# Gate and norm columns turned into rows through TensorE and 512-byte runs in DRAM, with the loads placed later

## The chip, the cores and the metric

One core of a Trainium2 chip runs the kernel. The metric is the device time of one execution in microseconds (us), and each kernel is run several times. TensorE (PE) does the matrix products and the transposes, VectorE (DVE) and ScalarE (ACT) the element work, GpSimd (POOL) a few powers, and SyncE (SP) issues every DMA of this kernel, in order, from one queue. An instruction that must wait holds up everything behind it on its engine.

## The reference, cut to what matters

A two-layer diffusion trunk: 512 latent tokens and 256 context tokens of 1024 channels, in float32. Layer 0 mixes tokens by attention, layer 1 by pooling, and each is followed by a gated feed-forward with 2816 hidden channels.

```python
m = (sc @ w_mod[i] + b_mod[i]).reshape(B, N_MOD, D_MODEL)
shift_m, scale_m, gate_m, shift_f, scale_f, gate_f = [m[:, k] for k in range(N_MOD)]
h = modulate(rmsnorm(x, g_pre_mix[i]), shift_m, scale_m)          # h * (1 + scale) + shift
...                                                                # mixer: y
x = x + gate_m * rmsnorm(y, g_post_mix[i])
h = modulate(rmsnorm(x, g_pre_ffn[i]), shift_f, scale_f)
x = x + gate_f * rmsnorm(conv_ffn(h, w_up[i], conv_w[i], conv_b[i], w_down[i]), g_post_ffn[i])
```

The vectors m have 1024 entries for each layer. The change concerns how five products of them, all functions of the channel alone, get from one layout to another.

## The kernel before, in words

Each float32 product is made of three matmuls on high and low parts (`mm3`, L122 to L124). The parts of a weight come from a 512 KB load into a `raw` buffer (two of them), a cast on ACT (L128, `whi`) and a subtraction on DVE (L129, `wlo`), with five buffers for each part.

A modulation vector is computed in eight chunks of 128 channels (`mod_chunk`): a 512 KB load of `w_mod` on SP (L184) and one reduction of the load on DVE (L186), which leaves the chunk as a column of `mods`, channel p of the chunk on partition p. These chunks are background work: a list `bg`, from which `background(n)` pops n steps at places in the attention, in the first up-projection (`up`) and in the first down-projection (`down` with `each0`). After the last chunk of a gate, `gate_col` multiplies the column by the norm's gain into `Gcol`; `gain_col` makes `Acol` in the same way.

A pre-norm on transposed data uses the columns as they are. A post-norm (`post_norm`, L247) works with tokens on partitions and needs the 1024 channels as a row on every partition. `to_row` (L203) does that: it stores the 128 x 8 column to DRAM with its two dimensions exchanged (L206), so that neighbouring channels, which lie on different partitions, come to lie side by side, and loads the 1024 channels back, the same row to all 128 partitions (L207). It is called five times in the code for `Grow`, `Gm1`, `Arow` and `Brow`, and once more for the last `Grow`:

- L481, in the attention, for `Grow` of the first post-norm;
- L790, in the first up-projection, for `Grow` of the first feed-forward;
- L907, at the step c = 0, kk = 10 of the first down-projection, for `Gm1` (it lies in `cvt`, the buffer of the up-projection's activations), followed by `pool_bias`;
- L910 and L911, at c = 1, kk = 5, for `Arow` and `Brow`, in slots that hold gated activations until then;
- L932, after the second up-projection (`up7`), for `Grow` of the last post-norm.

`pool_bias` (L808) loads `psr` and two rows of `bpr`, multiplies them on DVE (L815) and splits the product (L816, L817). A down-projection has two halves c of the output channels; for each of 11 weight blocks kk it multiplies four token tiles t, into bank `B2[t][c]`.

The order of the code isn't the order on the engines. A planner takes the code's instructions, follows their dependencies in a model of time and issues on each engine the earliest ready one, so that a step stands where the model finds its inputs and its buffer free, often long ahead of its place in the code. The order so found is fixed in the program.

Of the kernel before, what the change touches and what calls it, by code (L numbers as in the profile page):

```python
# [11 lines left out]
F32 = mybir.dt.float32  # L12
# [5 lines left out]
P = 128  # L18
D = 1024
SEQ = 512  # L20
CTX = 256
KT = D // P
# [9 lines left out]
FT = DFF // P  # L32
# [17 lines left out]
def trunk(ctx: ExitStack, tc: tile.TileContext, a, out: bass.AP):  # L50
    nc = tc.nc
    V, S, G, T = nc.vector, nc.scalar, nc.gpsimd, nc.tensor
# [7 lines left out]
    dram = ctx.enter_context(tc.tile_pool(name="dram", bufs=2, space=bass.MemoryType.DRAM))  # L60
# [23 lines left out]
    def flat(z):  # L84
        return z.rearrange("p a b -> p (a b)")
# [8 lines left out]
    ident = const.tile([P, P], F32, name="ident")  # L94
# [13 lines left out]
    mods = const.tile([P, 2, 6, KT], F32, name="mods")  # L108
    cmods = const.tile([P, 2, KT], F32, name="cmods")
    Acol = const.tile([P, 2, 2, KT], F32, name="Acol")  # L110
    Acx = const.tile([P, KT], F32, name="Acx")
    Gcol = const.tile([P, 2, 2, KT], F32, name="Gcol")
    scrow = rows("scrow", 60)
    Grow = big.tile([P, D], F32, name="Grow")
    cvt = slots("cvt", 62, 2, F32)
    h32 = big.tile([P, KT, P], F32, name="h32")
# [29 lines left out]
    def row_tile(name):  # L146
        return work.tile([P, D], F32, tag="row", name=name)
# [34 lines left out]
    def mod_chunk(i, v, j):  # L182
        raw = mraw[0]()
        nc.sync.dma_start(out=raw, in_=a["w_mod"][i, v, j])  # L184
        bias = bmod[:, i, v, j:j + 1]
        V.tensor_tensor_reduce(raw, raw, scrow, 1.0, bias, ALU.mult, ALU.add, mods[:, i, v, j:j + 1])  # L186

    def mod_vector(i, v, then=None):
        def last():
            mod_chunk(i, v, KT - 1)  # L190
            if then is not None:
                then()
        return [lambda j=j: mod_chunk(i, v, j) for j in range(KT - 1)] + [last]

    def gain_col(i, n):

        V.scalar_tensor_tensor(Acol[:, i, n, :], mods[:, i, 3 * n + 1, :], 1.0, gcols[:, n, i, :],
                               op0=ALU.add, op1=ALU.mult)

    def gate_col(i, n):  # L200
        V.tensor_mul(Gcol[:, i, n, :], mods[:, i, 3 * n + 2, :], gcols[:, 2 + n, i, :])

    def to_row(dst, col):  # L203

        d = dram.tile([KT, P], F32, tag="bounce", name="bounce")
        nc.sync.dma_start(out=d.rearrange("j p -> p j"), in_=col)  # L206
        nc.sync.dma_start(out=dst, in_=d.rearrange("j p -> (j p)").unsqueeze(0).broadcast_to([P, D]))  # L207

    bg = []

    def background(n):
        for _ in range(min(n, len(bg))):
            bg.pop(0)()


    hT = slots("hT", 0, 2 * KT)
# [77 lines left out]
    cols = small.tile([P, KT, 2], F32, name="cols", bufs=1)  # L294
# [50 lines left out]
    for j in range(KT):  # L345
# [5 lines left out]
        if j % 2 == 0:  # L351
            i = 28 + 2 * j
            wkv.append(load_w(a["w_qkv"][2, j // 2], 2, (rows(f"wkvh{j}", i, dt=F32R), rows(f"wkvl{j}", i + 2, dt=F32R))))
        f = slice(j * P, (j + 1) * P)
# [123 lines left out]


    mraw[0] = lambda: wp.tile([P, 1024], F32, tag="raw", name="mraw", bufs=2)  # L480
    bg += mod_vector(0, 2, lambda: (gate_col(0, 0), to_row(Grow, Gcol[:, 0, 0, :])))  # L481
    bg += mod_vector(0, 3) + mod_vector(0, 4, lambda: gain_col(0, 1))

    banks.close()
# [13 lines left out]
    def tp_next():  # L498
        tp_n[0] += 1
        return tp_ps[tp_n[0] % 2]  # L500
# [55 lines left out]
    for i in range(len(heads) + DEPTH):  # L556
# [4 lines left out]
        if i < len(heads):  # L561
# [8 lines left out]
            elif len(wo) < 8:  # L570
                n = len(wo)
# [7 lines left out]
        if i == len(heads) + 1:  # L579
# [3 lines left out]
            B2 = [[z[:, :512], z[:, 512:]] for z in W2]  # L583
# [14 lines left out]
    B2 = [[z[:, :512], z[:, 512:]] for z in W2]  # L598
# [39 lines left out]

    SPLIT = 4

    def up7(i, a32, mid, tail, early=2):

# [20 lines left out]
        load = lambda f: [load_w(a["w_up"][i, f, n], KT) for n in range(2)]  # L665
# [71 lines left out]
        for f in range(SPLIT, FT + 1):  # L737
            g = f - 1 if f > SPLIT else None
            new = f < FT
            if new:  # L740
                if f == SPLIT:
                    weights(f)
                row = row_tile("gates")
                rows_of[f] = (row[:, :512], row[:, 512:768])
                af, bc = A[(f - SPLIT) % 4], W2[f % 2]
                prod(af[:, :256], f, 1, True)
                S.copy(row[:, 0:256], af[:, :256])
            if g is not None:
                ag, bg_ = A[(g - SPLIT) % 4], W2[g % 2]
                gate, s5 = rows_of.pop(g)  # L750
                prod(ag[:, :256], g, 7, False)
                V.tensor_add(ag[:, 256:], ag[:, :256], s5)
            if new:
                prod(bc[:, :256], f, 2, True)
            if g is not None:
                prod(bg_[:, 512:768], g, 3, False)
                g2 = gate.rearrange("p (a b) -> p a b", a=2)
                V.tensor_add(g2, bg_.rearrange("p (a b) -> p a b", a=2)[:, :, :256], g2)
                act(g, gate)
            if new:  # L760
                prod(af[:, :256], f, 6, False)
                S.copy(row[:, 256:512], af[:, :256])  # L762
            if g is not None:
                prod(ag[:, :256], g, 4, False)
                V.scalar_tensor_tensor(a32[g], ag, -1.0, a32[g], op0=ALU.mult, op1=ALU.mult)
                W.pop(g)
            if new:
                prod(bc[:, 512:768], f, 5, True)
                S.copy(row[:, 512:768], bc[:, 512:768])
            if f + 1 < FT:  # L770
                weights(f + 1)
            if f >= FT - 3:
                tail(f - FT + 3)

    LAST = 6
    EARLY = FT - 2 * LAST
# [10 lines left out]

    a0 = gated("a0")
    mraw[0] = lambda: row_tile("mraw")
    bg += mod_vector(0, 5, lambda: (gate_col(0, 1), to_row(Grow, Gcol[:, 0, 1, :])))  # L790
    bg += mod_vector(1, 0) + mod_vector(1, 1, lambda: gain_col(1, 0))
    bg += mod_vector(1, 2, lambda: gate_col(1, 0))
    bg += mod_vector(1, 3) + mod_vector(1, 4, lambda: gain_col(1, 1))
# [4 lines left out]
    Gm1 = flat(cvt)  # L798
    hall = slots("hall", 52, KT, F32)
    wpl_dst = [[rows(f"wpl{n}{z}", i + 2 * z, dt=F32R) for z in range(2)] for n, i in enumerate((16, 20))]  # L800
    Arow, Brow = rows("Arow", 24), rows("Brow", 26)
# [6 lines left out]
    def pool_bias():  # L808

        ps, b = row_tile("psr"), row_tile("bpr")  # L810
        nc.sync.dma_start(out=ps, in_=a["pool_scale"].broadcast_to([P, D]))
        V.memset(b, 0.0)
        nc.sync.dma_start(out=b[0:1, :], in_=a["b_pool"])
        nc.sync.dma_start(out=b[32:33, :], in_=a["b_pool"])
        V.tensor_mul(b[0:33, :], b[0:33, :], ps[0:33, :])  # L815
        S.copy(bp, b)  # L816
        V.tensor_sub(bp[32:33, :], b[32:33, :], F(bp[32:33, :]))  # L817
        return ps
# [47 lines left out]
    def mixed(t):  # L866
        pre_norm(t, B2[t], mixrow[t], Acol[:, 1, 1], mods[:, 1, 3], hall[:, :, t * P:(t + 1) * P])
# [29 lines left out]
            mix(2)  # L897
            mix(3)

    ps_row = []  # L900

    def each0(c, kk):
        background(2)
        if c == 0 and kk == 8:
            background(100)
        if c == 0 and kk == 10:
            to_row(Gm1, Gcol[:, 1, 0, :])  # L907
            ps_row.append(pool_bias())
        if c == 1 and kk == FT // 2 - LAST:
            to_row(Arow, Acol[:, 1, 0, :])  # L910
            to_row(Brow, mods[:, 1, 0, :])  # L911
            pool_weights(ps_row[0])

    def down(i, aT, done, each, last, dst=(), order=(2, 3, 0, 1)):
# [8 lines left out]
    a32 = [place(f"a32{f}", gated_slot(1, f), (512,), F32) for f in range(FT)]  # L923
# [4 lines left out]
            for half in range(2):  # L928
                split(a1[half][f][:, 0, :], a1[half][f][:, 1, :], a32[f][:, half * 256:(half + 1) * 256])

    up7(1, a32, lambda: (mixed(2), mixed(3)), split_pair)
    to_row(Grow, Gcol[:, 1, 1, :])  # L932

    def finish(t):
        row = row_tile("outrow")
# [91 lines left out]
```

## Time and profile before

| | |
|---|---|
| median of 3 runs | 1067.87 us (1063.73 to 1069.53) |
| the profiled execution | 1074.04 us, its span 1072.3 us |
| granted TensorE clock, mean | 0.977 of full speed |
| PE busy | 997.8 us, 93% of the span |
| DVE busy | 747.6 us, 70% |
| ACT busy | 511.4 us, 48% |
| DMA moved | 143.70 MB in 46778 packets, 11122 of them under 512 bytes |

The stages of the span: modulation, the first pre-norm and the key, value and query products to about 110 us; attention to about 300 us; the first up-projection to about 544 us, the first down-projection to about 660 us; pooling mixer to about 720 us; then the second feed-forward. In the traces a line "start, length, engine, line" is an instruction or several merged ones; the bracket behind it gives how long its engine was idle before it and what ended that.

### The profile page before, as it was taken

What the parts mean: (1) busy time and instruction counts of PE and PEld (TensorE: products, weight loads), DVE (VectorE), ACT (ScalarE), POOL (GpSimd) and SP (SyncE); (2) the same over time, 40 slices, a digit from 0 to 9 for tenths busy, and PEclk for the clock granted to TensorE, in tenths of its full rate; (3) what the DMA queues carried; (4) which work ended last, traced back from release to release, by engine and by line L of the source; (5) the groups of instructions that cost most, each with busy time, mean ns of one, the idle gap of its engine ahead of it and who ended that gap; (6) DMA issues with size and microseconds to landing.
All of it is one profiled execution on the core that took longest, in us unless ns stands there. A gap on an engine that the chain in (4) does not pass through costs nothing.

```text
span 1072.3 us, 14605 instructions
## 1 busy us (share of the span) xinstructions
PE 997.8 (93%) x5586; PEld 862.9 (80%) x5586; DVE 747.6 (70%) x1259; ACT 511.4 (48%) x986; POOL 37.5 (3%) x55
## 2 busy tenths in 40 slices
PE   0898889999979999989999999899999999999997
PEld 0666678788878888878888887788999999988885
DVE  3988777896777999565542236889799999982214
ACT  5658578865624333244331223555455555761111
POOL 2003000000000000000000001110000000000000
PEclk9999899999989999989999999989999999999999
DMA  8543431352189989744333353411132332043312
GB/s 316 193 150 98 154 92 70 118 159 77 40 274 247 335 316 338 134 104 138 98 114 102 99 180 106 133 45 40 60 118 81 118 107 91 21 157 99 99 59 78
DMA packets 46778, 143.70 MB, mean 134 GB/s; under 512 B 11122, under 2 KB 11506, under 8 KB 46708
## 3 DMA queue, kind: packets, MB, share of 16 engines
q1 hardware_dynamic: 46708, 142.77, 41.4%
q8 instruction: 43, 0.70, 0.3%
q14 instruction: 27, 0.22, 0.1%
HBM read 140.63 MB, written 2.12 MB: 133 GB/s over the span
## 4 chain that ended last, share of the span: by engine, by line
PE 56%; DVE 18%; DMA 12%; ACT 8%; issue 4%; POOL 2%; SPq 0%; DVEq 0%; ACTq 0%; POOLq 0%
PE b L124 11%; PE b L122 11%; PE b L123 11%; PE b L733 5%; DMA mraw<-in_w_mod 5%; PE b L734 5%; DVE mraw L186 5%; PE b L735 5%; DVE wlo L129 3%; DMA raw<-in_w_up 2%; POOL rr L151 2%; DMA bpr<-in_b_pool 1%; DMA bounce<-Gcol 1%; DMA raw<-in_w_o 1%; DVE x L254 1%
## 5 line engine op out<-in xcount | busy, mean ns | idle before, releaser
L129 DVE TENSOR_TENSOR wlo<-raw,whi 128x1024 fp32r<-128x1024 f32 x105 | 128.0, 1223 | 150.2 <-ACT whi L128 150.0
L128 ACT CAST whi<-raw 128x1024 fp32r<-128x1024 f32 x105 | 110.1, 1053 | 178.9 <-PE b L124 105.1
L122 PE MATMUL b<-hT,whi 128*128 128x512 f32 (+1 forms) x480 | 175.5, 367 | 7.4 <-ACT hT L128 5.2
L123 PE MATMUL b<-hT,whi 128*128 128x512 f32 (+1 forms) x480 | 175.5, 366 | 0.6 <-DVE hT L129 0.6
L124 PE MATMUL b<-hT,wlo 128*128 128x512 f32 (+1 forms) x480 | 175.4, 366 | 0.6 <-DVE wlo L129 0.6
L122 PE MATMUL b<-whi,a 128*128 128x512 f32 x320 | 124.6, 390 | 0.8 <-ACT whi L128 0.8
L123 PE MATMUL b<-wlo,a 128*128 128x512 f32 x320 | 124.6, 389 | 0.3 <-DVE wlo L129 0.3
L124 PE MATMUL b<-whi,a 128*128 128x512 f32 x320 | 124.4, 389 | 0.0
L186 DVE CUSTOM_DVE_ANT_0 mraw<-mraw,scrow,bmod 128x1024 f32<-128x1024 f32 x80 | 101.2, 1281 | 14.8 <-DMA mraw<-in_w_mod 14.6
L122 PEld LDWEIGHTS b<-hT,whi 128*128 128x128 f32 x480 | 92.4, 193 | 22.3 <-ACT hT L128 5.6
L124 PEld LDWEIGHTS b<-hT,wlo 128*128 128x128 f32 x480 | 92.4, 193 | 15.1 <-DVE wlo L129 1.3
L123 PEld LDWEIGHTS b<-hT,whi 128*128 128x128 f32 x480 | 92.4, 192 | 15.0 <-DVE hT L129 1.1
L733 PE MATMUL b<-hT,whi 128*128 128x256 f32 x288 | 81.9, 285 | 0.1
L735 PE MATMUL b<-hT,wlo 128*128 128x256 f32 x288 | 81.5, 283 | 0.0
L734 PE MATMUL b<-hT,whi 128*128 128x256 f32 x288 | 81.4, 283 | 0.0
L151 POOL TENSOR_TENSOR rr<-rv,mhalf 128x1 f32<-128x1 f32 (+2 forms) x48 | 36.7, 768 | 1029.4 <-DVE rv L169 854.6
L122 PEld LDWEIGHTS b<-whi,a 128*128 128x128 f32 x320 | 60.0, 188 | 13.9 <-ACT whi L128 1.2
L123 PEld LDWEIGHTS b<-wlo,a 128*128 128x128 f32 x320 | 60.1, 188 | 13.3 <-DVE wlo L129 0.7
L124 PEld LDWEIGHTS b<-whi,a 128*128 128x128 f32 x320 | 60.1, 188 | 12.2
L733 PEld LDWEIGHTS b<-hT,whi 128*128 128x128 f32 x288 | 55.2, 192 | 1.0 <-ACT gates L762 0.9
L734 PEld LDWEIGHTS b<-hT,whi 128*128 128x128 f32 x288 | 55.2, 192 | 0.0
L735 PEld LDWEIGHTS b<-hT,wlo 128*128 128x128 f32 x288 | 55.2, 192 | 0.0
(307 smaller groups left out, 2162.4 us busy)
## 6 DMA issues: line engine op xcount, KB each, us to landing
mraw<-in_w_mod SPq DMA_DIRECT2D x96, 512.0 KB, 5.1
raw<-in_w_up SPq DMA_DIRECT2D x52, 512.0 KB, 4.0
raw<-in_w_down SPq DMA_DIRECT2D x44, 512.0 KB, 3.4
upv<-in_w_up SPq DMA_DIRECT2D x18, 512.0 KB, 4.1
upg<-in_w_up SPq DMA_DIRECT2D x18, 512.0 KB, 3.5
raw<-in_w_qkv SPq DMA_DIRECT2D x12, 512.0 KB, 4.3
raw<-in_w_o SPq DMA_DIRECT2D x8, 512.0 KB, 3.5
x<-in_x SPq DMA_DIRECT2D x4, 512.0 KB, 10.0
```

The costliest lines, as they stand in the source:

```text
L122: T.matmul(ps, lh, rh, start=first, stop=False)
L123: T.matmul(ps, lh, rl, start=False, stop=False)
L124: T.matmul(ps, ll, rh, start=False, stop=last)
L128: S.copy(hi, src)
L129: V.tensor_sub(lo, src, F(hi))
L151: G.tensor_tensor(r[:, :n], v, mhalf[:, :n], op=ALU.pow)
L186: V.tensor_tensor_reduce(raw, raw, scrow, 1.0, bias, ALU.mult, ALU.add, mods[:, i, v, j:j + 1])
L254: V.scalar_tensor_tensor(xc, row[:, HALVES[c]], r, xc, op0=ALU.mult, op1=ALU.add)
L733: T.matmul(ps, lhs[0], rhs[0], start=first and k == 0, stop=False, skip_group_check=True)
L734: T.matmul(ps, lhs[0], rhs[1], start=False, stop=False, skip_group_check=True)
L735: T.matmul(ps, lhs[1], rhs[0], start=False, stop=last, skip_group_check=True)
```

## The change

`to_row` is replaced by `to_rows`. It takes one or more columns, transposes each on TensorE into eight rows of 128 channels in a PSUM bank, copies these with ACT into part of the tile `h32`, and stores them to DRAM so that each run is 512 bytes. It returns the loads as functions, and the callers place them. The load of the first row stands at least three background steps after its store in the code (`later`). The other five columns are made at one place, c = 0, kk = 10 of the first down-projection, four in one store and one in another, through the banks `B2[0][1]` and `B2[1][1]`. The loads of `Grow` and `Gm1` stand at c = 1, kk = 2, those of `Arow` and `Brow` where they stood, and the last load of `Grow` in the middle of `up7`.

```diff
-    def to_row(dst, col):
-
-        d = dram.tile([KT, P], F32, tag="bounce", name="bounce")
-        nc.sync.dma_start(out=d.rearrange("j p -> p j"), in_=col)
-        nc.sync.dma_start(out=dst, in_=d.rearrange("j p -> (j p)").unsqueeze(0).broadcast_to([P, D]))
-
-    bg = []
+    def to_rows(ps, cols):
+
+        n = len(cols)
+        for c, col in enumerate(cols):
+            T.transpose(ps[0:KT, c * P:(c + 1) * P], col, ident)
+        stage = h32[0:KT, 0:n, :]
+        S.copy(stage, ps[0:KT, :n * P].rearrange("j (n p) -> j n p", n=n))
+        d = dram.tile([n, KT, P], F32, tag="bounce", name="bounce")
+        nc.sync.dma_start(out=d.rearrange("n j p -> j n p"), in_=stage)
+        return [lambda dst, c=c: nc.sync.dma_start(
+            out=dst, in_=d[c].rearrange("j p -> (j p)").unsqueeze(0).broadcast_to([P, D])) for c in range(n)]
+
+    bg, later = [], []
 
     def background(n):
         for _ in range(min(n, len(bg))):
             bg.pop(0)()
+            if later:
+                later[0][0] -= 1
+                if later[0][0] < 0:
+                    later.pop(0)[1]()
...
-    bg += mod_vector(0, 2, lambda: (gate_col(0, 0), to_row(Grow, Gcol[:, 0, 0, :])))
+
+    def mix_gate():
+        gate_col(0, 0)
+        load, = to_rows(tp_next(), [Gcol[:, 0, 0, :]])
+        later.append([3, lambda: load(Grow)])
+
+    bg += mod_vector(0, 2, mix_gate)
...
+            if f == FT // 2:
+                midway()
...
-    bg += mod_vector(0, 5, lambda: (gate_col(0, 1), to_row(Grow, Gcol[:, 0, 1, :])))
+    bg += mod_vector(0, 5, lambda: gate_col(0, 1))
...
         if c == 0 and kk == 10:
-            to_row(Gm1, Gcol[:, 1, 0, :])
+            row_loads.extend(to_rows(B2[0][1], [Gcol[:, 0, 1, :], Gcol[:, 1, 0, :], Acol[:, 1, 0, :], mods[:, 1, 0, :]]))
+            row_loads.extend(to_rows(B2[1][1], [Gcol[:, 1, 1, :]]))
             ps_row.append(pool_bias())
+        if c == 1 and kk == 2:
+            row_loads[0](Grow)
+            row_loads[1](Gm1)
         if c == 1 and kk == FT // 2 - LAST:
-            to_row(Arow, Acol[:, 1, 0, :])
-            to_row(Brow, mods[:, 1, 0, :])
+            row_loads[2](Arow)
+            row_loads[3](Brow)
             pool_weights(ps_row[0])
...
-    up7(1, a32, lambda: (mixed(2), mixed(3)), split_pair)
-    to_row(Grow, Gcol[:, 1, 1, :])
+    up7(1, a32, lambda: (mixed(2), mixed(3)), split_pair, lambda: row_loads[4](Grow))
```

## Rows read from the trace of the kernel before

**Rows 1.** The page: busy time by engine; PE's busy tenths in 40 slices of 26.8 us

```profile
PE 997.8 (93%) x5586; PEld 862.9 (80%) x5586; DVE 747.6 (70%) x1259; ACT 511.4 (48%) x986; POOL 37.5 (3%) x55
...
PE   0898889999979999989999999899999999999997
```

**Rows 2.** Windows, attention: stretch, its length, busy time by engine, granted clock, DMA, GB/s

```profile
145.00:150.00 5.00, 5.00 (x31) 4.27 (x30) 4.24 (x11) 4.02 (x15) 1.01 (x1) 1.00 0.20 26
150.00:155.00 5.00, 4.44 (x33) 3.87 (x32) 1.45 (x4) 4.17 (x10) 0.00 (x0) 1.00 0.75 233
155.00:160.00 5.00, 0.39 (x2) 0.40 (x3) 2.67 (x6) 0.00 (x0) 0.00 (x0) 0.87 0.25 48
160.00:165.00 5.00, 5.00 (x18) 4.13 (x17) 2.32 (x7) 3.19 (x7) 0.00 (x0) 0.50 0.23 90
165.00:170.00 5.00, 5.00 (x35) 4.37 (x35) 2.45 (x5) 2.43 (x5) 0.00 (x0) 0.94 0.02 5
```

**Rows 3.** Timeline of SP in the attention: start, length, line, transfer

```profile
139.15 0.39 SPq L206 DMA_DIRECT2D bounce<-Gcol  x1
140.29 0.34 SPq L133 DMA_DIRECT2D raw<-in_w_o  x1
151.09 0.33 SPq L207 DMA_DIRECT2D Grow<-bounce  x1
151.51 0.38 SPq L184 DMA_DIRECT2D mraw<-in_w_mod  x1
```

**Rows 4.** Timelines of DVE and PE behind that, with the idle time before each

```profile
157.32 1.28 DVE L186 CUSTOM_DVE_ANT_0 mraw<-mraw,scrow,bmod 128x1024 f32<-128x1024 f32 x1 [5.87 <-DMA mraw<-in_w_mod]
...
159.61 0.90 PE L525 MATMUL tp<-ident,p 128*128 128x128 f32 x3 [5.17 <-DVE qT L129]
```

**Rows 5.** DMA issues of 139 to 152 us: transfer, count, KB, median us to landing

```profile
raw<-in_w_o SPq DMA_DIRECT2D x1, 512.0 KB, 12.0
```

**Rows 6.** Line 206, all six stores: from issue to landing

```profile
DMA to landing us min/median/max: 10.8/13.5/17.0
```

**Rows 7.** Timeline of SP in the first up-projection

```profile
435.35 0.44 SPq L206 DMA_DIRECT2D bounce<-Gcol  x1
...
446.54 0.38 SPq L206 DMA_DIRECT2D bounce<-Gcol  x1
447.01 0.43 SPq L813 DMA_DIRECT2D bpr<-in_b_pool  x1
```

**Rows 8.** Timeline of DVE behind that

```profile
461.78 1.22 DVE L815 TENSOR_TENSOR bpr<-bpr,psr 33x1024 f32<-33x1024 f32 x1 [13.76 <-DMA bpr<-in_b_pool]
```

**Rows 9.** Windows, first up-projection, columns as in the second group

```profile
463.00:466.00 3.00, 0.82 (x4) 0.40 (x3) 2.46 (x4) 2.97 (x5) 0.00 (x0) 0.99 0.00 0
466.00:470.00 4.00, 3.42 (x8) 2.15 (x8) 3.80 (x5) 1.33 (x3) 0.00 (x0) 0.50 0.40 116
470.00:480.00 10.00, 10.00 (x40) 8.11 (x39) 6.77 (x10) 5.96 (x10) 0.00 (x0) 0.86 0.51 163
```

**Rows 10.** Windows around the second store of line 206, same columns

```profile
310.00:320.00 10.00, 7.03 (x35) 6.86 (x36) 8.88 (x16) 3.58 (x7) 0.00 (x0) 0.54 0.84 274
320.00:330.00 10.00, 10.00 (x76) 9.59 (x75) 6.78 (x11) 1.74 (x3) 0.00 (x0) 1.00 1.06 206
```

**Rows 11.** Timeline of SP, last load of Grow

```profile
684.89 0.33 SPq L207 DMA_DIRECT2D Grow<-bounce  x1
```

**Rows 12.** Tile tp: a line's durations min/median/max in ns, first and last start

```profile
L525 PE MATMUL tp<-ident,p x192: 270/272/477, 124.3 to 290.9; 128*128 128x128 f32 x192
```

**Rows 13.** DMA issues after 1050 us, stores of the output

```profile
out_x<-x SPq DMA_DIRECT2D x8, 256.0 KB, 2.0
```

**Rows 14.** Waits of SP's queue, 540 to 640 us: total, times, longest

```profile
SPq L133 <- DVE wlo L129: 66.0, 14, 5.4
```

**Rows 15.** Timeline of ACT in the first down-projection

```profile
600.46 1.06 ACT L128 CAST whi<-raw 128x1024 fp32r<-128x1024 f32 x1 [4.38 <-PE b L124]
```

**Rows 16.** Windows, first down-projection, columns as in the second group

```profile
600.00:610.00 10.00, 10.00 (x45) 8.26 (x44) 2.45 (x2) 2.11 (x2) 0.00 (x0) 1.00 0.23 73
```

More of the change, by code (lines that the diff above doesn't have):

```diff
@@ L639, in trunk, with up7 @@
     SPLIT = 4
-    def up7(i, a32, mid, tail, early=2):
+    def up7(i, a32, mid, tail, midway, early=2):
         def act(f, gate):
@@ L898, in after_ffn0 @@
             mix(3)
-    ps_row = []
+    ps_row, row_loads = [], []
     def each0(c, kk):
```

## The prediction

> **What bounds the kernel now.** PE is busy for 93% of the span [rows 1], so a stall elsewhere costs time only where PE runs dry behind it. I therefore looked first at where the change works, the stores and loads of L206 and L207 on SP, then at what stood behind each on SP, then at DVE and PE there, and last at the windows, which say whether PE stopped and what its clock was afterwards.
>
> Two places show a chain from such a store to an idle PE. The first is in the attention. The store of `Gcol` goes out at 139.15, a weight load at 140.29, and then the queue stands until 151.09, when the load of `Grow` may read what was stored; only then does the next `mraw` load go, at 151.51 [rows 3]. DVE has that chunk next in its order and is idle for 5.87 us until it lands; PE needs what DVE does after it and is idle for 5.17 us [rows 4]. When PE resumes, it does so at half clock, the lower of its two levels, for about five microseconds [rows 2].
>
> The second is in the up-projection. Three stores go out from 435.35 on and a fourth at 446.54, right ahead of the two small `bpr` loads [rows 7]. Those are 4 KB each, yet DVE waits for them for 13.76 us, until 461.78 [rows 8], and its weight parts are missing when PE gets to them: PE is idle between 463 and 470 and at half clock again [rows 9].
>
> What makes the stores slow? The six land 10.8 to 17.0 us after their issue [rows 6], while 256 KB of output in longer runs land in 2.0 us [rows 13]. The 512 KB weight load issued 1.1 us behind the first store takes 12.0 us [rows 5], although only 26 GB/s move in the meantime [rows 2]. So a store in 4-byte pieces (1024 of them) holds up whatever is queued behind it for some 11 us, not because the DMA engines are full of bytes. I take the piece length as the cause.
>
> **The change, part by part.** Sums go against the profiled execution (span 1072.3 us, 1074.0 with what lies around it), which is 6.2 us above the median of the runs; I carry that difference over.
>
> *First store and load (attention).* The wait of SP goes. Without it `mraw` can be issued shortly after 140.3 instead of 151.5 and land before DVE asks for it at 151.4 (157.32 less 5.87). Gain, from the windows [rows 2]: idle PE 0.56 + 4.61 = 5.2 us, and of the clock 5.0 x (1 - 0.50) + 5.0 x (1 - 0.94) = 2.8 us, together 8.0 us. What is late next: PE was full at 145 to 150 with DVE at 4.24 of 5 us [rows 2], so PE should stay the limit.
>
> What comes in is a longer chain: `Gcol`, a transpose on PE, a copy on ACT, the store. PE and ACT wait in order for it, and behind the store on SP stand the weight load and `mraw`. The transpose is 0.27 us [rows 12], the copy about half of the 1.06 us that a cast of 1024 columns takes [rows 15], plus what stands ahead of it on ACT. The new store's landing isn't in the trace; bounds are 2.0 [rows 13] and 17.0 us [rows 6]. I take 2.0, since its runs are 512 bytes and it has 8 of them. SP is then free for `mraw` at about 143.5 even if the load stands right behind the store; the slack until DVE starves is 151.4 - 5.8 (landing of this `mraw`) = 145.6, so 2 us remain. Cost: nothing, and the 8.0 us come back in part if that slack is used up.
>
> *Later loads.* The planner moves steps: the last `Grow` store of the code stands after the second up-projection and goes out at 446.54 [rows 7], its load at 684.89 [rows 11], as soon as its buffer is free. So the delays written into the code may hold on no engine. I count nothing for them, neither for the first load nor for the one in `up7`: the first needs no delay at a landing of 2 us, and the last ran ahead without one.
>
> *Second store (feed-forward gate, 322 us).* PE is full at full clock behind it [rows 10], so its removal is worth nothing, and the cover is PE's own work; the idle time before 320 precedes the store.
>
> *The four stores at 435 to 447.* They can't stay there. Their transposes go into banks that the up-projection's last two blocks still use, so they can't run before those have been read, shortly ahead of 544 us, where that stage ends. Then nothing slow stands ahead of `bpr`, DVE's 13.76 us shrink to the few microseconds of a small load, and the weight parts are in time. Gain [rows 9]: idle 2.18 + 0.58 = 2.8 us, clock 3.42 x 0.50 + 10.0 x 0.14 = 3.1, together 5.9 us. Behind it PE is busy for 90% or more of each of the next seven slices, 482 to 670 us [rows 1], so the gain is kept.
>
> *Five transposes, two copies, two stores in the down-projection.* PE is full there [rows 16], so its work adds: the transposes cost 0.27 us each alone [rows 12] and less in a row, where they overlap (three took 0.90 us even at half clock [rows 4]); with the one in the attention I take 1.2 us for six. By the Trainium skill ("TensorE: Matmul & The Clock Gate", part 4) one takes about 275 ns in a kernel, so 1.65 us for six, an estimate; the row has the same duration, and the difference is only their overlap. The copies, 0.6 us each, lie in ACT's 4.38 us of idle time per weight [rows 15].
>
> A wait is added: both copies use the same part of `h32`, so the second, on ACT, waits until the first store has landed, and PE's first product into `B2[1][1]` waits for that copy. The store may itself stand behind a weight load that waits up to 5.4 us [rows 14]. Worst: 5.4 + 2.0 + 0.6 = 8.0 us, less the tile in between (6 matmuls at 10.0 us for 45 [rows 16], 1.3 us) = 6.7 us idle, plus 3 us of clock as in the other two gaps. Best: nothing, where the planner puts the other tiles or weight blocks ahead. ACT's casts behind the waiting copy are four weights ahead of PE, so they don't suffer. I take 1 us, near the lower end, since the planner knows this wait and PE has other ready work.
>
> **Sum.** 1074.0 - 8.0 - 5.9 + 1.2 + 1.0 = 1062.3 us, less 6.2 = 1056 us against the median of 1067.9.
>
> **The rivals.** *One gap stays.* In the attention DVE waits for `mraw` at other times too, and PE now waits for the transpose; the gap may only shrink. With the second gap alone: 1067.9 - 5.9 + 2.2 = 1064; with the first alone 1062. For it: the slack of 2 us. Against it: the stall has one clear head. I give 1063.
>
> *Given back.* PE also stops at 300 to 320, with the clock down to 0.54 [rows 10]. That stretch waits for modulation chunks and a norm, and work that arrives earlier may just wait longer there: 8 us of the first gap are lost, partly the second: 1066.
>
> *The store stays slow.* If the landing doesn't come from the pieces but from the write to DRAM or from what is queued, the new one takes 10.8 to 17.0 us as well. Then the first gap stays, the second goes, and the wait in the down-projection is 5.4 + 13.5 + 0.6 - 1.3 = 18 us of idle PE, with 3 of clock: 1067.9 - 5.9 + 1.2 + 18 to 21 = 1081 to 1084 at worst, about 1076 with a part covered by reordered tiles. With both gaps gone it decides from about 10 us of idle PE at that place (10 + 3 = 13.9 - 1.2). Against it: 2.0 us [rows 13] for a store to DRAM. The Trainium skill ("DMA: Bandwidth & Descriptors", Bandwidth) goes by size: 4 KB take 0.68 us and all under 64 KB is dominated by descriptors, there on GpSimd's path. Taken by size alone the old store's 10.8 us would have to be queueing, and this rival would hold; the count of descriptors, 1024 against 8, is the reading that the rows bear out.
>
> *It doesn't do what it says.* The loads aren't later, as argued; at a landing up to about 4 us this gives the same 1056 to 1058.
>
> **How the numbers follow.** Forecast, with the last rival: 0.62. One gap stays: 0.18. Given back: 0.11. Store stays slow: 0.09. A measurement of this kernel tells apart about 0.5%, 5.3 us; faster means under 1062.5. That is the forecast and about half of the second case: 0.70; slower 0.09; the rest, 0.21, within. The range: the low end is all of 13.9 us without the costs, less the 4 us by which single runs lie below the median: 1050. The high end is the third case, 1066, which also takes in the worst of the added wait (9.7 us in place of 1).
>
> **What would show it.** Right: SP without a stand of 10 us behind `bounce`, landings of 2 to 4 us, DVE L186 without the 5.87 us, L815 with under 4 us, no clock of 0.50 at either place. Wrong: `bounce` landings over 5 us; a PE wait on ACT between the two halves of the down-projection; a new DVE wait for `mraw`; more idle time at 300 to 320.

## The result and the profile after

The kernel after takes 1057.35 us (1056.28 to 1059.54, six runs), the kernel before on the same chip 1068.74 us (1063.73 to 1072.84, six runs): a ratio of 0.9898 [0.9871, 0.9926]. Measured again later, beside the last experiment, it was 1057.51 against 1073.33 us, 0.9852 [0.9825, 0.9879]. The profiled execution of after takes 1057.91 us with a span of 1056.1 us, 16.1 us less than that of before.

The page of after: engines, the granted clock in 40 slices of 26.4 us, and packets. Beside [rows 1] PE has 7 us less of busy time for six more instructions, and the packets under 512 bytes are 4906 where they were 11122:

```profile
PE 990.8 (94%) x5592; PEld 857.4 (81%) x5592; DVE 747.5 (71%) x1259; ACT 512.9 (49%) x989; POOL 37.4 (4%) x55
...
PEclk9999899999989999999999999899999999999999
...
DMA packets 40611, 143.71 MB, mean 136 GB/s; under 512 B 4906, under 2 KB 5338, under 8 KB 40540
```

Windows of after, with the columns of [rows 2]: the attention, the first up-projection and the first down-projection. They answer to [rows 2, 9 and 16]:

```profile
140.00:150.00 10.00, 10.00 (x70) 9.07 (x69) 8.61 (x20) 8.41 (x25) 1.01 (x1) 1.00 0.31 104
150.00:160.00 10.00, 10.00 (x69) 8.77 (x69) 6.83 (x15) 7.74 (x16) 0.00 (x0) 1.00 0.18 54
160.00:170.00 10.00, 10.00 (x65) 8.87 (x64) 8.53 (x18) 9.88 (x28) 1.01 (x1) 1.00 0.08 18
...
450.00:460.00 10.00, 10.00 (x46) 8.29 (x45) 4.47 (x7) 4.03 (x6) 0.00 (x0) 1.00 0.30 102
460.00:470.00 10.00, 10.00 (x46) 8.29 (x45) 4.43 (x7) 4.01 (x6) 0.00 (x0) 1.00 0.32 105
...
600.00:610.00 10.00, 10.00 (x45) 8.27 (x45) 3.68 (x3) 1.05 (x1) 0.00 (x0) 1.00 0.72 261
```

Both gaps are gone: PE is full in both places and the granted clock stays at its upper level. In the third place, where the change added its work, PE is full too.

The timeline of SP in after (start, length, line, transfer) answers to [rows 3 and 7]:

```profile
138.87 0.33 SPq L133 DMA_DIRECT2D raw<-in_w_o  x1
142.51 0.33 SPq L184 DMA_DIRECT2D mraw<-in_w_mod  x1
...
180.83 0.35 SPq L211 DMA_DIRECT2D bounce<-h  x1
182.07 0.35 SPq L212 DMA_DIRECT2D Grow<-bounce  x1
...
595.35 0.30 SPq L211 DMA_DIRECT2D bounce<-h  x1
...
598.23 0.32 SPq L211 DMA_DIRECT2D bounce<-h  x1
598.61 0.33 SPq L212 DMA_DIRECT2D Grow<-bounce  x1
```

No store stands at 139 or at 435 to 447 any more. `mraw` goes out 3.6 us behind the weight load, where it was 11.2 us. The first store goes only at 180.83, and the load that reads it follows 1.24 us later: the store has landed by then. DVE's steps that waited, in its timeline of after, start without an idle time ahead of them, where [rows 4 and 8] show 5.87 and 13.76 us:

```profile
149.94 1.28 DVE L186 CUSTOM_DVE_ANT_0 mraw<-mraw,scrow,bmod 128x1024 f32<-128x1024 f32 x1
...
428.45 1.21 DVE L833 TENSOR_TENSOR bpr<-bpr,psr 33x1024 f32<-33x1024 f32 x1
```

The new work, in the timelines of PE and of ACT in after: the first transpose, one of the later five, and the second copy, behind its wait for the first store of the down-projection.

```profile
179.01 0.27 PE L207 MATMUL tp<-ident,Gcol 128*8 128x128 f32 x1
...
593.82 0.27 PE L207 MATMUL b<-ident,Acol 128*8 128x128 f32 x1
```

```profile
596.91 0.26 ACT L209 COPY h<-b 8x128 f32<-8x128 f32 x1 [0.63 <-DMA bounce<-h]
```

To see where the time went I took the start of the same instructions out of the traces: the transposes of p in the attention (L525 of before), products of the first up- and down-projection, and the mixer's products with `band`. Times of before in us, then each kernel's difference to it; the kernels e1 to e10 are those of the next section, and e8 is before once more:

```
                     before   after     e1     e2     e3     e6     e7     e8     e9    e10
p-transpose 32       147.54   -1.43  -4.33  -1.52  -1.27  -1.77  -1.73  -1.46  -4.06  -2.35
p-transpose 64       178.90   -9.32 -12.24  -3.62  -9.18  -1.63  -3.73  -3.08 -11.96 -10.24
p-transpose 128      221.71  -11.28 -12.00  -3.48  -5.04  -1.62  -5.52  -3.18 -12.06 -11.70
up-proj. product 500 397.16  -11.34 -12.54  -3.96  -7.13  -1.48  -7.72  -3.52 -11.88 -11.51
first down-proj.     551.12  -17.53 -11.21 -10.14 -13.31  -7.66 -13.31  -3.01 -18.06 -17.69
band first           656.71  -17.34 -11.24  -9.24 +11.35  -7.75 -10.88  -1.38 -17.74 -17.04
band last            692.09  -15.90 -11.25  -9.26 +11.35  -6.32  -7.88  -1.37 -16.30 -17.05
end                 1072.26  -16.13  -9.85  -7.38 +10.67  -5.23  -8.96  -1.69 -15.86 -15.70
```

A difference below zero is an earlier start; what a kernel wins in a stretch is what its difference falls by from one line to the next. After wins 7.9 us between the 32nd and the 64th transpose, the place of the first gap, and 2.0 more by the 128th; nothing between 222 and 397 us; 6.2 in the place of the second gap. It loses 0.2 us over the down-projection and 1.4 in the pooling mixer.

### The profile page after: what moved, and what is told of

Read it like the earlier page. It is cut to its first block, busy times and chain, and to the rows that moved or that the text cites. A ratio compares the mean times of both kernels' runs of the same rounds, so it can differ in the third digit from the quotient of the medians.

```text
span 1056.1 us, 14619 instructions
## 1 busy us (share of the span) xinstructions
PE 990.8 (94%) x5592; PEld 857.4 (81%) x5592; DVE 747.5 (71%) x1259; ACT 512.9 (49%) x989; POOL 37.4 (4%) x55
## 2 busy tenths in 40 slices
DMA packets 40611, 143.71 MB, mean 136 GB/s; under 512 B 4906, under 2 KB 5338, under 8 KB 40540
## 4 chain that ended last, share of the span: by engine, by line
PE 75%; DVE 8%; ACT 7%; DMA 5%; issue 3%; POOL 2%; SPq 0%; DVEq 0%; ACTq 0%; POOLq 0%
PE b L122 16%; PE b L124 16%; PE b L123 16%; PE b L749 6%; PE b L751 5%; PE b L750 5%; DMA mraw<-in_w_mod 2%; POOL rr L151 2%; PE tp L541 1%; DVE wlo L129 1%; DVE mraw L186 1%; ACT whi L128 1%; DVE x L264 1%; DMA raw<-in_w_up 1%; PE sc L122 1%
```

## The experiments

Ten experiments ran, e1 to e4, e5 to e8, and e9 with e10 each beside one another on one chip, with runs of before between them. Lines are numbered by each kernel's own code.

**The first row alone.** The kernel after, with the other five columns stored as before:

```diff
+    def to_row(dst, col):
...
-    bg += mod_vector(0, 5, lambda: gate_col(0, 1))
+    bg += mod_vector(0, 5, lambda: (gate_col(0, 1), to_row(Grow, Gcol[:, 0, 1, :])))
...
+            to_row(Gm1, Gcol[:, 1, 0, :])
...
+            to_row(Arow, Acol[:, 1, 0, :])
+            to_row(Brow, mods[:, 1, 0, :])
...
+    to_row(Grow, Gcol[:, 1, 1, :])
```

> Only the first row (Grow of the attention's post-norm) goes through TensorE and a 512-byte store; the other five columns are stored in 4-byte pieces as before. Theory (two separate gaps, each with its own store): the gap at 150 to 170 us goes, the one at 463 to 480 stays, 8 us below the kernel before, about 1061; DVE L186 without the wait of 5.87 us, DVE L815 with its 13 to 14 us. Rival (one gap stays where work is given back): within 3 us of before.

It took 1064.69 us (1058.88 to 1068.37, ten runs), a ratio to before of 0.9932 [0.9905, 0.9959]. In its windows the first gap is gone, and the second is there, larger than in [rows 9]:

```profile
150.00:160.00 10.00, 10.00 (x66) 8.56 (x65) 5.85 (x12) 7.74 (x23) 0.00 (x0) 1.00 0.12 48
...
450.00:455.00 5.00, 0.96 (x5) 0.46 (x3) 2.39 (x3) 1.65 (x4) 0.00 (x0) 0.79 0.24 16
455.00:460.00 5.00, 3.60 (x8) 2.47 (x9) 4.93 (x7) 2.58 (x4) 0.00 (x0) 0.52 0.25 70
```

Its list of waits (total, times, longest) has 17.0 us of DVE for `bpr`, where [rows 8] has 13.76:

```profile
DVE bpr L839 <- DMA bpr<-in_b_pool: 17.0, 1, 17.0
...
PE b L122 <- ACT whi L128: 5.6, 2, 5.0
```

So one part of the gain stands without the other; the wait for `bpr` is within what before itself shows (17.5 us in its second profile, below). Between the 500th product and the down-projection this kernel loses 1.3 us to before's first profile, where before's second loses 0.5: at most a part of what the first gap brings is waited off in the second, as long as that is there.

**The other rows alone.** The kernel after, with the first column stored as before:

```diff
+    def to_row(dst, col):
...
-        load, = to_rows(tp_next(), [Gcol[:, 0, 0, :]])
-        later.append([3, lambda: load(Grow)])
+        to_row(Grow, Gcol[:, 0, 0, :])
```

> The first row is stored in 4-byte pieces as before; the other five columns go through TensorE in the first down-projection. Theory: the wait of SP of about 10 us in the attention stays with 5 us of idle PE and 5 us of half clock behind it; no slow store stands ahead of bpr; 5.9 us for that gap, less nearly nothing for the added work, so about 6 us below the kernel before, 1062 to 1063. The sum of this gain and that of the run with the first row alone is that of the whole change, 11.4 us, within 2. Rival (added work in the down-projection costs 2 us): 4 us below.

1066.83 us (1063.12 to 1068.40, ten runs), a ratio of 0.9944 [0.9918, 0.9970]. SP stands again between store and load, the waits are those of [rows 4], and the windows show the first gap and a full PE in the place of the second:

```profile
137.64 0.39 SPq L218 DMA_DIRECT2D bounce<-Gcol  x1
...
149.38 0.33 SPq L219 DMA_DIRECT2D Grow<-bounce  x1
```

```profile
155.00:160.00 5.00, 2.85 (x11) 2.46 (x12) 4.50 (x9) 2.27 (x4) 0.00 (x0) 0.76 0.33 105
...
420.00:480.00 60.00, 60.00 (x266) 49.69 (x265) 36.75 (x52) 23.03 (x34) 0.00 (x0) 1.00 0.36 116
```

The two parts give 8.3 and 6.1 us by the medians beside before's 1072.95. Their sum, 14.4, is 3.0 us more than the 11.4 that the expectation allowed 2 us around. It lies between the 11.4 and the 15.8 us that the whole change gave in its two measurements, so within what before itself varies they add up.

**The same kernel with its stores in 4-byte pieces.** The kernel after, in which only the order of the numbers in DRAM is another, so that each store falls into pieces of one number and the rows hold their channels in another order; the transposes, copies, loads and their order on every engine are those of after:

```diff
-        d = dram.tile([n, KT, P], F32, tag="bounce", name="bounce")
-        nc.sync.dma_start(out=d.rearrange("n j p -> j n p"), in_=stage)
+        d = dram.tile([n, P, KT], F32, tag="bounce", name="bounce")
+        nc.sync.dma_start(out=d.rearrange("n p j -> j n p"), in_=stage)
...
```

> The changed kernel with one thing other: the three stores write the same elements in 4-byte pieces (1024, 4096 and 1024 of them) in place of 512-byte runs, so the loaded rows have their channels in another order; all engines have the same instructions in the same order. Theory (the number of pieces sets the landing, about 11 us for 1024, and holds up the queue behind): the first store lands 11 us or later, SP stands for that long at 181 us and PE stops there as it did at 154; the second takes some 45 us, the weights of the down-projection come late by more than the four that are ahead (22 us), and PE is idle there for 20 us or more: 25 to 45 us slower than the changed kernel. Rival (the new place and the late loads are what helps, not the length of the runs): within 3 us of the changed kernel.

1084.80 us (1084.11 to 1088.58, four runs): 27 us above after, and slower than before, 1.0141 [1.0098, 1.0185]. The first store, 1024 pieces from eight partitions, holds SP from 181.01 to 189.02, 8.0 us:

```profile
181.01 0.34 SPq L211 DMA_DIRECT2D bounce<-h  x1
189.02 0.35 SPq L212 DMA_DIRECT2D Grow<-bounce  x1
```

The second, of 4096 pieces, is what the second copy waits for, and PE waits for that copy, as the list of waits and the windows show:

```profile
ACT h L209 <- DMA bounce<-h: 21.5, 1, 21.5
...
PE b L122 <- ACT h L209: 19.7, 1, 19.7
```

```profile
600.00:610.00 10.00, 2.60 (x12) 1.81 (x10) 1.54 (x2) 0.49 (x1) 0.00 (x0) 0.73 0.45 3
610.00:620.00 10.00, 0.00 (x0) 0.00 (x0) 0.00 (x0) 0.00 (x0) 0.00 (x0) 0.50 0.75 25
620.00:630.00 10.00, 7.74 (x28) 6.31 (x29) 2.45 (x2) 1.31 (x2) 0.00 (x0) 0.74 0.50 87
```

The expectation missed the sizes, 11 and 45 us where 8.0 and about 22 were measured, and the path: it had PE run out of weights, and PE waited for the copy. By the table the two stores cost 6.1 us (64th to 128th transpose, -9.18 to -5.04, where after goes from -9.32 to -11.28) and 24.5 us (first down-projection to `band`, +24.66, where after has +0.19). Of the 6.1 us, about 4.1 are left by the 500th product (-7.13 beside -11.34).

**The loads at once.** The kernel after without the delays of its loads:

```diff
-        later.append([3, lambda: load(Grow)])
+        load(Grow)
...
-    up7(1, a32, lambda: (mixed(2), mixed(3)), split_pair, lambda: row_loads[4](Grow))
+    up7(1, a32, lambda: (mixed(2), mixed(3)), split_pair, lambda: None)
+    row_loads[4](Grow)
```

> The changed kernel with its loads directly behind their stores in the code, the last one behind the second up-projection as before, so without the delays. Theory (the planner places them by their buffers, and the short store lands in under 2 us): same time as the changed kernel within 1 us, with the first load at the same place on SP. Rival (the delays matter): SP stands behind a store, and up to 8 us of the gain are lost.

1058.90 us (1058.77 to 1059.53, four runs), 0.9894 [0.9848, 0.9941]; the first load goes out at 182.13, in after at 182.07. The median is 1.4 to 1.6 us above the two of after, which ran beside other runs of before; the ratios to before agree, so the delays do nothing here that can be measured.

**Runs of 64 bytes.** The kernel after with stores in runs of 16 numbers, eight times as many as in after; here too the rows hold their channels in another order:

```diff
+        d = dram.tile([n, 8, KT, 16], F32, tag="bounce", name="bounce")
+        nc.sync.dma_start(out=d.rearrange("n b j q -> j n b q"), in_=stage.rearrange("j n (b q) -> j n b q", q=16))
...
```

> The changed kernel with its stores in pieces of 64 bytes (64, 256 and 64 of them), so the loaded rows have their channels in another order. Theory (landing goes with the number of pieces, 5 to 8 ns each as in the run with 4-byte pieces, on top of about 1.3 us): the first store lands in under 2 us, the second in about 3 us, PE's wait for the second copy stays hidden; within 1 us of the changed kernel. Rival (any run under 512 bytes is slow): the first store takes several us and part of the gap in the attention returns, 3 us or more slower.

1057.08 us in two runs (1057.07 and 1057.09), 0.9856 [0.9794, 0.9917]. The first store (64 pieces) goes at 179.90 and its load at 181.23, at most 1.33 us to land; the second (256 pieces) goes at 594.49, and the copy that waits for it starts at 596.41, 1.92 us later, in ACT's timeline:

```profile
596.41 0.25 ACT L209 COPY h<-b 8x128 f32<-8x128 f32 x1 [1.00 <-DMA bounce<-h]
```

**The column stores kept, their loads moved.** The kernel before with the places of the change for its loads in the code, and without transposes:

```diff
...
+        for c, col in enumerate(cols):
+            nc.sync.dma_start(out=d[c].rearrange("j p -> p j"), in_=col)
...
+        load, = to_rows(None, [Gcol[:, 0, 0, :]])
+        later.append([3, lambda: load(Grow)])
```

> The kernel before with the change's placing of the loads in the code, but with columns stored in 4-byte pieces and without TensorE. Theory (the stores hold up the queue behind them, and the planner places loads by their buffers): both gaps stay; within 3 us of the kernel before, the stores still about 11 us to landing. Rival (it is the load right behind the store that blocks SP, and a later load lets the next transfers through): the first gap goes, 6 to 8 us below before.

1067.65 us (1061.11 to 1069.97, ten runs), 0.9945 [0.9918, 0.9972]. In the attention the edit changed nothing: up to 322 us every engine has the instructions of before in their order, and on SP the load of `Grow` (148.51) still stands between the weight load and `mraw` (148.93). The first gap stays, with 5.4 us of PE's waiting, but the rival, that it is the load behind the store that blocks SP, isn't tested there. Further on the loads did move: the store at 332.00 has its load only at 432.11, and yet three 512 KB loads whose landing the trace has, issued 1.4, 6.3 and 7.5 us behind it, take 9.5 to 11.7 us, where the median of such loads in before's page is 5.1. That speaks for the store itself holding up what is queued behind it; how much of the first gap is the load's stand on SP stays open. The second gap is gone, against the expectation, although the slow stores still stand ahead of `bpr` on SP:

```profile
428.17 2.94 SPq L208 DMA_DIRECT2D bounce<-mods  x1
...
438.89 0.89 SPq L208 DMA_DIRECT2D bounce<-Gcol  x1
439.87 5.62 SPq L828 DMA_DIRECT2D bpr<-in_b_pool  x1
```

```profile
150.00:160.00 10.00, 4.64 (x26) 3.88 (x25) 4.13 (x8) 3.58 (x8) 0.00 (x0) 0.85 0.48 151
...
440.00:480.00 40.00, 40.00 (x179) 33.11 (x178) 21.98 (x29) 16.27 (x25) 0.00 (x0) 1.00 0.51 136
```

The planner had put the instructions in another order. Two weight loads, not one, go out between the third of these stores and the fourth; DVE waits 9.3 us for a weight and then, by its list of waits, only 1.9 us for `bpr`:

```profile
DVE bpr L830 <- DMA bpr<-in_b_pool: 1.9, 1, 1.9
```

The second gap is therefore no certain consequence of the slow stores, but of them together with the order around them.

**The bias loaded early.** The kernel before, its six stores unchanged, with the product of `pool_bias` loaded and computed early in the first up-projection, into `h32`:

```diff
+    def bias_early():
+        s = row_tile("psr")
+        nc.sync.dma_start(out=s, in_=a["pool_scale"].broadcast_to([P, D]))
+        V.memset(b, 0.0)
+        nc.sync.dma_start(out=b[0:1, :], in_=a["b_pool"])
+        nc.sync.dma_start(out=b[32:33, :], in_=a["b_pool"])
+        V.tensor_mul(b[0:33, :], b[0:33, :], s[0:33, :])
+    up(0, a0, lambda f: (background(2), bias_early() if f == 5 else None), lambda: last_norm(B2[3]))
...
-        V.tensor_mul(b[0:33, :], b[0:33, :], ps[0:33, :])
```

> The kernel before with all its 4-byte stores where they were, and with b_pool and a second copy of pool_scale loaded and multiplied early in the first up-projection, so that at 447 us nothing on DVE waits for a load issued behind a store. Theory (the second gap is DVE's wait for bpr, with everything behind it on DVE): the gap at 463 to 480 us goes, 5 to 6 us below before. Rival (the weight loads behind the four stores come late by themselves, 15 us to landing): PE still stops there, within 2 us of before.

1065.28 us (1062.56 to 1070.09, ten runs), 0.9937 [0.9913, 0.9961]. The stores go at 435.80 to 447.39, nearly as in [rows 7], ACT still waits up to 10.1 us for a weight behind them, and PE stops for no more than 0.3 us:

```profile
ACT whi L128 <- DMA raw<-in_w_up: 37.3, 13, 10.1
```

```profile
450.00:460.00 10.00, 10.00 (x46) 8.29 (x45) 1.65 (x2) 1.73 (x2) 0.00 (x0) 1.00 1.13 101
460.00:470.00 10.00, 9.70 (x43) 7.74 (x42) 4.90 (x8) 4.13 (x6) 0.00 (x0) 1.00 0.42 102
```

It wins 5.6 us in that place (-7.72 to -13.31). So the second gap is DVE's wait for `bpr` and what queues behind it on DVE; the late weight loads alone are covered. Of the 5.6 us it loses 5.4 again between the down-projection and the mixer's end, for which I have no cause. So the 7.9 us by the medians aren't that gap's alone: 5.5 us of this profile's lead stand at the 128th transpose already, ahead of the edit, where up to 313 us every engine has the instructions of before in their order.

**Before once more**, unchanged, one more profiled execution:

> The kernel before, one more profiled execution. Theory (the profile of before that the prediction rests on showed a larger second gap than most executions): the same two gaps, the second with another length, DVE L815 waiting 10 to 17 us; a span of 1064 to 1075 us. Rival (the gaps are the same in each execution): both within 0.5 us of the first profile.

1072.35 us. Its waits, beside the 13.76 and 5.17 us of [rows 8 and 4]:

```profile
DVE bpr L815 <- DMA bpr<-in_b_pool: 17.5, 1, 17.5
...
PE tp L525 <- DVE qT L129: 4.8, 3, 4.1
```

The gaps have no fixed size: the first is 1.1 us shorter here, and DVE's wait in the second 3.7 us longer.

**The short store alone.** The kernel before with one thing changed: its stores write each partition's eight numbers in one run of 32 bytes. There is no transpose, no copy and no moved load, and every engine has the instructions of before in their order:

```diff
-        d = dram.tile([KT, P], F32, tag="bounce", name="bounce")
-        nc.sync.dma_start(out=d.rearrange("j p -> p j"), in_=col)
-        nc.sync.dma_start(out=dst, in_=d.rearrange("j p -> (j p)").unsqueeze(0).broadcast_to([P, D]))
+        d = dram.tile([P, KT], F32, tag="bounce", name="bounce")
+        nc.sync.dma_start(out=d, in_=col)
+        nc.sync.dma_start(out=dst, in_=d.rearrange("p j -> (p j)").unsqueeze(0).broadcast_to([P, D]))
```

> The kernel before with one thing changed: its six stores write each partition's eight values as they lie, 32 bytes in one run, 128 runs from 128 partitions instead of 1024 pieces of 4 bytes; the rows come out with their channels in another order. No transpose, no copy, no later load; every engine has the same instructions in the same order as before. Theory (the count of pieces is what holds the queue): the stores land in about 2 us (256 pieces took 1.9 us from eight partitions), the first load of Grow goes under 3 us behind its store, PE has no wait of 4 to 5 us at about 159 us, DVE waits under 5 us for bpr, both gaps go, and the time is that of after without its costs, 1056 to 1060 us, ratio to before 0.985 to 0.991. Rival (pieces under 512 bytes stay slow when they come from 128 partitions, or the form of a column store does it): landings stay at 5 us or more, and the time stays within 4 us of before. Rival (the gain needs the other order that the change brings, and the short store alone gives only the first gap): 1063 to 1066 us.

Beside it ran the kernel after:

> The kernel after unchanged, beside the run above on the same chip. Theory: 1056 to 1060 us, and the runs lie within 4 us of each other, as both gaps that varied from run to run in before are gone. If the short runs from 128 partitions are as good, the two kernels lie within 2 us; if the transposes, copies and the added wait cost what the prediction took (2.2 us), this one is about 2 us the slower. Rival: in before the landing, not the gap, scatters, and after scatters by 10 us here as well.

The short store alone takes 1057.51 us (1055.25 to 1058.93, four runs), 0.9848 [0.9814, 0.9882]; after takes 1057.51 us (1056.34 to 1058.34, four runs); before 1073.33 us (1069.41 to 1076.17, seven runs). SP's timeline in the first of the two:

```profile
135.10 0.33 SPq L206 DMA_DIRECT2D bounce<-Gcol  x1
136.24 0.33 SPq L133 DMA_DIRECT2D raw<-in_w_o  x1
136.66 0.38 SPq L207 DMA_DIRECT2D Grow<-bounce  x1
139.86 0.33 SPq L184 DMA_DIRECT2D mraw<-in_w_mod  x1
...
423.32 0.32 SPq L206 DMA_DIRECT2D bounce<-Gcol  x1
424.39 0.31 SPq L813 DMA_DIRECT2D bpr<-in_b_pool  x1
```

And its windows:

```profile
150.00:160.00 10.00, 10.00 (x66) 8.51 (x65) 5.77 (x13) 7.73 (x22) 0.00 (x0) 1.00 0.12 47
...
440.00:480.00 40.00, 40.00 (x178) 33.14 (x177) 18.54 (x26) 15.10 (x23) 0.00 (x0) 1.00 0.30 95
```

Its page counts 5746 packets under 512 bytes, 5376 fewer than before's: six times 1024 less 128, as the edit has it. Line 206 in it, all six stores, from issue to landing, beside the 10.8, 13.5 and 17.0 us of [rows 6]:

```profile
DMA to landing us min/median/max: 1.4/3.9/5.3
```

The load of `Grow` follows its store after 1.56 us, where [rows 3] have 11.9. Both gaps are gone, and the end comes 15.9 us earlier than in before's profile, as in after. With the run on 4-byte pieces this settles the cause from both sides: the pieces alone, put into after, make it slower than before; fewer pieces alone, put into before, give all that the change gave. In both pairs every engine has the same instructions in the same order. The stores have the same bytes, so fewer pieces are longer pieces too; the pair doesn't tell count from length. Runs of this length leave the channels in another order, which is what the transposes are for.

## Why the prediction held

**The time.** 1056 us was forecast and 1057.35 measured, within 1050 to 1066, and faster came. The closeness is in part luck, however. The sum made the profiled execution 11.7 us shorter, to 1062.3; it became 16.1 us shorter. And the 6.2 us by which the profile of before lay above its median were carried over; that of after lies 0.6 above its own. The first error made the forecast too long, the second too short. Of the 4.4 us by which the sum fell short, 1.4 stand ahead of the first gap and 2.0 behind it, up to the 128th transpose; 0.3 are the second gap's; 2.0 are costs that were counted and didn't come; the mixer took 1.4 back, and its end gave 0.2. What was carried over probably belonged to the gaps themselves: the kernels with both gaps gone scatter little (after by 3.3 and 2.0 us, the short store alone by 3.7, the loads at once by 0.8), those with one gap left by 5 to 10, before by 7 to 12 us within one set of runs, and its gaps differ from profile to profile. In the later measurement the medians differ by 15.8 us, near the profile's 16.1.

**First gap, 8.0 us.** Right in mechanism and size: 7.9 us by the 64th transpose, 9.9 by the 128th; against the other profile of before 6.3 and 8.1. Five profiles have before's instructions in this stretch (before twice, the other rows alone, the columns kept with their loads moved, the bias loaded early); from the 32nd to the 128th transpose after takes 6.1 to 10.0 us less than they do, 8.1 in the middle of the five. The stretch ahead of it, which the change doesn't touch, starts 1.4 to 4.3 us earlier in several kernels and evens out by the 128th transpose, where the four of the table that have no slow store by then lie at -11.3 to -12.1; nearer than that the gap can't be sized.

**The longer chain in the attention.** This step failed in its place, without harm. I had the store at 139 to 143 us and `mraw` behind it with 2 us to spare. The transpose of a `Gcol` that is finished at 138 us ran at 179.01, where by the code it takes its turn on the two `tp` banks. So nothing stood ahead of `mraw`, and the slack was larger. The 4-byte pieces in after show what the store costs at 181 us if it is slow: 8.0 us on SP and 6.1 of time.

**Second gap, 5.9 us.** Right: 6.2. The step said that nothing slow would stand ahead of `bpr` and DVE's wait would shrink; it went to nothing [rows 8]. The bias loaded early shows that DVE's wait is the link, as the step had it. What the step didn't see is that the gap varies with the order: moving the loads alone removed it, with the slow stores left in place, and with the first gap won alone it was 1.3 us larger than in [rows 9], of which before's own second profile, with nothing changed, shows 0.5.

**Loads later, second store.** Right, both at nothing as far as the runs tell: with the loads at once the median is 1.55 us above that of after, inside the two ratios' intervals, and between the 128th transpose and the 500th product nothing is won or lost.

**Transposes, copies and the added wait, 1.2 + 1.0 us.** Too much: 0.2 us over the whole down-projection, with the five transposes 0.1 us apart where they follow each other (593.82, 593.92 and 594.03 in PE's timeline). The second copy waited for 0.63 us, and PE had other tiles meanwhile. The short store alone, which has none of this work, takes the same 1057.51 us. That the wait's upper bound was real is shown by the 4-byte pieces: 19.7 us of PE's time in that very place.

**The landing, 2.0 us.** A little high: at most 1.24 us for the first and 1.56 us for the second store (595.35 to 596.91).

**The rivals.** One gap stays: no, and the two halves, at 1064.69 and 1066.83 us, show how that would have looked. Given back: not at 300 to 320, but 1.4 us in the mixer or, in after's second profile, behind it; over that stretch the kernels differ by 0 to 3 us from one another, with no cause that I could name. The store stays slow: no. Its premise, that the landing comes from a write to DRAM as such or from what is queued, whatever its pieces, is refuted by the short store alone; its place and its order of size (18 us idle and 3 of clock) are what the 4-byte pieces gave, 24.5 us. It doesn't do what it says: true of the later loads, at no price.

**What stays open.** Why 1024 pieces take 10.8 to 17.0 us from 128 partitions [rows 6] and 8.0 us from eight. The trace says where the time isn't: in before's DMA view the pieces of the first store all start between 140.0 and 141.2 us (1040 packets under 512 bytes), none starts from 141.2 to 150, and the store lands at 151.07; on 4-byte pieces in after, all start before 184.0 and the load that waits for them goes at 189.02. What fills the 5 to 10 us behind the last piece no run here shows. Open too are what makes the mixer lose 1 to 3 us in some kernels, and what takes back 5.4 us where the bias is loaded early. Whether after could gain by placing its first transpose earlier wasn't tried; nothing waits for it. Nor was before with its slow store and a first load that stands later on SP.

## What to carry to other kernels

Look for small transfers by their number of pieces, not by their bytes: a 4 KB store of single numbers held up its queue for 11 us, three times what the 512 KB loads of `in_w_o` take to land in after (3.7 us, median of eight), and the price is paid by whoever's load stands behind it, here DVE and then PE with its clock. The cure is worth what the victims' gaps show in the windows, idle time and clock together; make it by any layout with fewer pieces (for the kernel's time, runs of 32 bytes were as good as 512), and check by that one change alone which part of a larger rewrite earns the gain. Where single runs of a kernel scatter by more than the change is worth, ask first whether the scatter belongs to the gap that is to go.

## What the hardware showed unexpectedly

A store of a few kilobytes lands fast as long as its pieces are few: 8 of 512 bytes in at most 1.24 us, 64 of 64 bytes in at most 1.33, 256 of 64 bytes in at most 1.92, 128 of 32 bytes in 1.4 us at the first gap's place (up to 5.3 elsewhere). With 1024 pieces of 4 bytes it is 8.0 us from eight partitions, with 4096 about 22 us. The time doesn't follow the bytes: 16 KB in 256 pieces take a quarter of what 4 KB in 1024 take. Four times as many pieces of 4 bytes took 2.8 times as long, but no store had many pieces longer than that, so a price for each piece and a price for very short ones aren't told apart. The Trainium skill ("DMA: Bandwidth & Descriptors", Specifications) names 512 bytes as the least transfer for the line rate; for stores of this size no run here shows a loss of the kernel's time down to 32 bytes, since a kernel with runs of 32 and one with runs of 512 both take 1057.51 us. The same page's advice (Rules for kernel authors) that a strided last dimension falls into one descriptor per element, and is to be made contiguous, agrees with the packets in the trace: before has 5376 packets under 512 bytes more than the kernel with 128 runs to a store, six times 1024 less 128.
